# Convolution module: scaled operands instead of scaled products, four taps on another engine, earlier polyphase copies

## The chip, the cores and the metric

The kernel runs on one core of one Trainium2 chip. The metric is the device time of one execution in microseconds, as the median of several runs. A core has five engines that work side by side, each on its own list of instructions and in the order of that list: TensorE (PE: matrix products; PEld is its weight load), VectorE (DVE), ScalarE (ACT), GpSimd (POOL) and SyncE (SP), which here only issues DMA transfers. Semaphores make an instruction wait for another engine's or for a transfer; what stands behind a waiting instruction on the same engine waits too.

## The reference

Two decoder layers on 512 tokens of 1024 features, in float32. The change touches only the mixer of the first layer, a causal Conformer convolution:

```
u = rms_norm(h, conv_norm_g)                      # h * g / rms(h), per token
a = u @ w_pw1 + b_pw1                             # 1024 -> 2048
u = a[..., :1024] * sigmoid(a[..., 1024:])        # gate
u = depthwise causal convolution(u, 31 taps) + dw_b
u = silu(layer_norm(u, ln_g, ln_b))
h = h + u @ w_pw2 + b_pw2
```

Behind it come a SwiGLU feed-forward block and a gated input embedding, then the second layer (differential attention, the same two blocks). None of that is changed.

## The kernel before

**Layout.** Features lie on the 128 partitions, tokens along the free axis, so the 1024 features are eight chunks of 128 x 512, numbered c = 0 to 7. Every float32 product is made of three faster ones: each operand is split into a rounded part ("hi", a cast on ACT) and its remainder ("lo", a subtraction), and `mm3` (lines 165 to 169) adds lo x hi, hi x hi and hi x lo in PSUM. A weight is loaded into `wraw` (two buffers), cast to `whi` on ACT (L160) and its remainder written to `wlo` (L162, on DVE, at some places on POOL).

**The norm.** `Norm.split` (L201, L202) splits h times the gain g without the token's factor 1/rms, so that TensorE can begin before the factor is known. The factor is formed meanwhile, spread over all partitions by a product (L277, PSUM tile `tp`) and copied to SBUF as `rb` (L249). It is applied to the products instead: per chunk DVE multiplies the gate's sum and the value's sum by `rb` (L612 and L618).

**The loop over the chunks** (lines 579 to 638). Chunk c forms two sums of 24 matmuls each, the gate `pg` and the value `pa`. DVE scales both, ACT takes the sigmoid (L613), and DVE forms the gated chunk `up` (L632, or L624 in polyphase order). Chunks 0 and 1 have their products ahead of the others, beside the start of the kernel.

**The 31 taps.** Chunks 1, 3, 5 and 6 (`PHASED`) run on TensorE in four phases: the gated chunk goes to DRAM and back (`pi`, L419 and L423), 36 small matmuls with banded matrices make the convolution (L462), `phased_out` copies the sum out of PSUM (L470, ACT), writes it to DRAM on ACT's queue (`po`, L472), reads it back in token order on SP's queue (L475), and `shift` adds a bias and a row `shrow` (L482, DVE). Chunks 0, 2, 4 and 7 run on DVE, one instruction to a tap (L518, `sc` in PSUM); some of their taps are made by ACT (L508) and added by POOL (L509). Of chunk 7, eight taps run on TensorE with diagonal matrices (L412). `BETWEEN` and `BEHIND` say which chunk's taps TensorE takes between or behind the sums of a later chunk. The row `shrow` comes from chunk 0 alone (`moments(0)`, L557 to L561): chunks 1 to 7 need it.

**The end of the convolution.** POOL adds the finished chunks up (`macc`, L575) and their squares (L571), TensorE turns the sums (L671), DVE reduces them (L693), and from there follow the layer norm, SiLU and the last product. While the last taps run, TensorE works on six of eight pieces of a product of the first layer's input embedding (`factor`, `project`), which serve as filling; the features for them are loaded and split in `pfeatures` (L360 to L362).

**Order.** A planner orders the instructions of each engine by its own estimate; `manual_schedule` pins some pieces (the start, chunk 7's taps on DVE and the end), and `issue_after` holds an instruction back until another. SBUF tiles with one tag share buffers: the operands `A0` to `A7` have one buffer each, `wk` has four, `wraw` two, `whi` and `wlo` four.

Of the kernel before, what the change touches and what calls it, by code (L numbers as in the profile page):

```python
# [13 lines left out]
F32R = mybir.dt.float32r  # L14
AF = mybir.ActivationFunctionType
ALU = mybir.AluOpType
# [4 lines left out]
P = 128  # L21
S = 512
D = 1024
NC = D // P
# [27 lines left out]
CUTS = 2  # L52


PE_TAPS = (0, 0, 0, 0, 0, 0, 0, 8)
POOL_TAPS = (10, 0, 11, 0, 11, 0, 0, 7)


# [33 lines left out]
def trunk(ctx, tc, xT, xtok, pT, wts, diag, dww, vec, rel, onehot, lamv, out):  # L92
# [9 lines left out]
    def sb(shape, tag, bufs, dt=F32):  # L102
        uid[0] += 1
        return pool.tile(shape, dt, tag=tag, name=f"{tag}_{uid[0]}", bufs=bufs)
# [17 lines left out]
    def col(name, i=0):  # L122
        a, _ = VEC[name]
        return vt[:, a + i : a + i + 1]
# [15 lines left out]
    t = tp()  # L140
# [49 lines left out]
    def both(t):  # L190
        return t[:, 0], t[:, 1]
# [12 lines left out]
    class Norm:  # L204
# [41 lines left out]
        def rows(self):  # L246

            r = sb([P, S], "rb", 1)
            last_rows[0] = A.copy(r, spread(self.dg))  # L249
            return r  # L250

    last_v = [None]
    last_pow = [None]
# [20 lines left out]
    def spread(dg):  # L274
        t = tp()
        if not isinstance(dg, tuple):
            last_spread[0] = T.matmul(t, ones, dg, start=True, stop=True)  # L277
            return t
        for i, d in enumerate(dg):
            T.matmul(t, ones_r, d, start=i == 0, stop=i == 1)  # L280
        return t
# [99 lines left out]
    accs = {}  # L381
    last_tap = [None]
    outs = {}
    shifts = []
    last_part = [None]
    outer = []
# [2 lines left out]
    def half(w):  # L389
        acc = mm()  # L390
        for k in range(NC):
            mm3(acc, wpart(w, k), norm.u[k], k == 0, k == NC - 1)
        return acc
# [73 lines left out]
    def phased_out(c):  # L467

        o = big()
        A.copy(o, accs[c])  # L470
        d = dram.tile([P, S], F32, tag=f"po{c}", name=f"po{c}")
        outs[c] = nc.scalar.dma_start(d, o)  # L472
        both_ = sb([P, 2, S], f"B{c}", 1)
        for g in range(NPH):
            nc.sync.dma_start(  # L475
                both_[g * FG : (g + 1) * FG, 1].rearrange("p (r n) -> p r n", r=NPH),
                bass.AP(d.tensor, d.offset + g * P, [[S, FG], [FG * S, NPH], [1, P]]),
            )
        tok = "p (n r) -> p n r"

        def shift():
            V.scalar_tensor_tensor(  # L482
                both_[:, 0].rearrange(tok, r=NPH), both_[:, 1].rearrange("p (r n) -> p n r", r=NPH), col("dw_b", c),
                shrow.rearrange(tok, r=NPH), ALU.add, ALU.add,
            )
            y[c] = both_[:, 0]

        if c < NC - 3:
            shift()
        else:  # L490
            shifts.append(shift)

    def other_taps(c, behind=None):
        if c in PHASED:
            return phased_out(c)
        up, acc = ups[c], accs[c]
        alone = c in ALONE
        tap = lambda j: up[:, j : j + S]
        a, b = PE_TAPS[c], PE_TAPS[c] + POOL_TAPS[c]
        pacc = wk()  # L500
        for j in range(a, b):
            if j == a:
                with tc.issue_after(outs[5].ins) if alone else nullcontext():
                    A.activation(pacc, tap(j), AF.Identity, scale=wt(c, j), bias=col("dw_b", c))
            else:
                pr = sb([P, S], f"C{2 + j % 2}", 2)
                with tc.issue_after(outs[6 if j == b - 1 else 5].ins) if alone else nullcontext():
                    A.activation(pr, tap(j), AF.Copy, scale=wt(c, j))  # L508
                last_part[0] = G.tensor_tensor(pacc, pacc, pr, ALU.add)  # L509
        yc = sb([P, 2, S], f"B{c}", 1)  # L510
        if c == 0:
            sums["acc"] = yc[:, 1]
        yc = yc[:, 0]
        sum_ = sc() if alone else acc

        def taps(js):
            for j in js:
                V.scalar_tensor_tensor(sum_, tap(j), wt(c, j), sum_, ALU.mult, ALU.add)  # L518

        if alone:  # L520
            with tc.manual_schedule(engines={V.engine}):
                V.scalar_tensor_tensor(sum_, tap(b), wt(c, b), shrow, ALU.mult, ALU.add)
                taps(range(b + 1, b + 3))
                shifts[0]()
                moments(NC - 3)
                taps(range(b + 3, KW - 2))
                shifts[1]()
                outer.append(weight(eng=G, after=(last_part[0], None)))
                taps(range(KW - 2, KW))
                moments(NC - 2)  # L530
                outer.append(weight(eng=G, after=(last_sq[0], None)))
                V.tensor_tensor(yc, sum_, pacc, ALU.add)
                V.tensor_tensor(yc, acc, yc, ALU.add)
                y[c] = yc
                moments(c)
            return
        with tc.issue_after(behind.ins) if behind else nullcontext():
            if c == 0:
                V.tensor_scalar(sum_, tap(b), wt(c, b), None, ALU.mult)
            else:  # L540
                V.scalar_tensor_tensor(sum_, tap(b), wt(c, b), shrow, ALU.mult, ALU.add)
        taps(range(b + 1, KW))
        V.tensor_tensor(yc, sum_, pacc, ALU.add)
        y[c] = yc
# [34 lines left out]
    for c in range(NC):  # L579
# [18 lines left out]
        if 0 < c < NC - 1:  # L598
            late = ((first_gate, last_rows[0]),) * 2 if c == 1 else ((None, None),) * 2
            pairs.append(tuple(weight(after=i) for i in late)[::-1])  # L600
            pair_loads.append(loaded[0])
        if c == 1:
            ph = pfeatures(0, [(sb([P, S], t, 2, F32R), sb([P, S], t, 2, F32R)) for t in ("wth", "wtl")])
        if c > 0:
            pg = half(wg) if c > 1 else g1
            for k in BETWEEN[c]:
                pe_taps(k)
            pa = half(wa) if c > 1 else a1
            for k in BEHIND[c]:
                pe_taps(k)  # L610
        tg, ta = big(), big()
        V.tensor_tensor(tg, pg, rb, ALU.mult)  # L612
        gated = A.activation(tg, tg, AF.Sigmoid, bias=col("b_pw1", 8 + c))  # L613
        if c == NC - 1:

            with tc.issue_after(gated.ins):
                A.activation(powers[:, 24:32], vt[:, :8], AF.Silu)
        scaled = V.tensor_tensor(ta, pa, rb, ALU.mult)  # L618
        if c == 0:
            first_gate = scaled  # L620
        if c in PHASED:
            up = big()
            phases, tok = "p (r n) -> p n r", "p (n r) -> p n r"
            formed = V.scalar_tensor_tensor(  # L624
                up.rearrange(phases, r=NPH), ta.rearrange(tok, r=NPH), col("b_pw1", c),
                tg.rearrange(tok, r=NPH), ALU.add, ALU.mult,
            )
            phased_in(c, up)
        else:
            up = ups[c] = sb([P, S + PAD], "C0", 2)  # L630
            G.memset(up[:, :PAD], 0.0)
            V.scalar_tensor_tensor(up[:, PAD:], ta, col("b_pw1", c), tg, ALU.add, ALU.mult)  # L632
# [950 lines left out]
```

## Time and profile before

| | |
|---|---|
| Time, median of 3 runs | 1237.82 us (1237.47 to 1237.89) |
| Time of the profiled execution | 1238.28 us, its span 1236.3 us |
| TensorE busy | 1224.5 us, 99% of the span |
| VectorE busy | 880.1 us, 71% |
| ScalarE busy | 625.1 us, 51% |
| GpSimd busy | 474.3 us, 38% |
| Granted TensorE clock | 0.999 |
| Convolution stage | from the start to about 160 us |

The profile's times are microseconds from the start of the span of one profiled execution. A row of the timeline gives the start, the length, the engine, the line and operation, the tile written and the tiles read, the sizes, how many instructions it merges (x) and, in brackets, the idle time just before and what ended it. Instructions on DVE and ACT follow each other a little faster than their length, since the end of one overlaps the start of the next; the distance from start to start is what one costs in a dense stretch. Busy time of TensorE is not time at its peak.

### The profile page before, as it was taken

How to read it: one execution, taken by the hardware profiler on the slowest of the kernel's cores; microseconds unless marked ns; L12 is line 12 of the kernel's file. 1: busy time of each engine (PE TensorE's matmuls, PEld its weight loads, DVE VectorE, ACT ScalarE, POOL GpSimd, SP SyncE). 2: the span in 40 equal slices, each digit the busy share in tenths (PEclk: the TensorE clock that was granted, in tenths of full speed). 3: DMA queues.
4: the chain of work that ended last, by engine and by line, in shares of the span. 5: the costliest groups of instructions: out<-in, count | busy, mean ns of one | idle time of the engine just before them, and what ended most of it. 6: DMA issues, size and time to landing. Idle time of an engine off the chain costs nothing.

```text
span 1236.3 us, 18296 instructions
## 1 busy us (share of the span) xinstructions
PE 1224.5 (99%) x7011; PEld 1072.4 (87%) x7011; DVE 880.1 (71%) x1251; ACT 625.1 (51%) x1099; POOL 474.3 (38%) x355
## 2 busy tenths in 40 slices
PE   9999999999999999999999999999999999999998
PEld 7888688888998899888788888888889998999887
DVE  5889866975895479547767776747966884588545
ACT  6563464533553255434657777735534552455432
POOL 0594813024670464133436636131026640562220
PEclk9999999999999999999999999999999999999999
DMA  8664323333333322334423321142243333233331
GB/s 328 224 209 144 106 68 110 93 106 119 93 96 119 102 86 73 116 105 153 125 85 105 99 86 53 56 150 85 90 132 90 100 120 108 80 103 86 105 99 69
DMA packets 50019, 138.44 MB, mean 112 GB/s; under 512 B 5731, under 2 KB 10851, under 8 KB 49932
## 3 DMA queue, kind: packets, MB, share of 16 engines
q1 hardware_dynamic: 47664, 133.71, 35.1%
q10 hardware_dynamic: 2268, 3.57, 1.0%
q8 instruction: 55, 0.90, 0.3%
q14 instruction: 32, 0.26, 0.1%
HBM read 130.94 MB, written 6.31 MB: 111 GB/s over the span
## 4 chain that ended last, share of the span: by engine, by line
PE 84%; DVE 7%; DMA 4%; issue 3%; ACT 1%; POOL 1%; SPq 0%; ACTq 0%; DVEq 0%; POOLq 0%
PE mm L167 26%; PE mm L168 26%; PE mm L169 26%; DMA wraw<-in_wts 2%; DVE sc L518 2%; PE mm L1282 1%; DVE wlo L162 1%; PE sc L1242 1%; PE tp L1269 1%; PE sc L1239 1%; PE sc L462 1%; DMA B<-po 1%; DVE wlo L863 1%; POOL wk L509 0%; PE tp L1190 0%
## 5 line engine op out<-in xcount | busy, mean ns | idle before, releaser
L160 ACT CAST whi<-wraw 128x1024 fp32r<-128x1024 f32 (+1 forms) x139 | 141.3, 1026 | 233.4 <-PE mm L169 108.5
L167 PE MATMUL mm<-A,wlo 128*128 128x512 f32 (+1 forms) x540 | 209.7, 388 | 0.7 <-ACT A L201 0.6
L162 DVE TENSOR_TENSOR wlo<-wraw,whi 128x1024 fp32r<-128x1024 f32 (+1 forms) x132 | 167.6, 1276 | 59.7 <-ACT whi L160 59.2
L168 PE MATMUL mm<-A,whi 128*128 128x512 f32 (+1 forms) x540 | 208.6, 386 | 0.0
L169 PE MATMUL mm<-A,whi 128*128 128x512 f32 (+1 forms) x540 | 206.6, 387 | 0.1
L167 PE MATMUL mm<-B,wlo 128*128 128x512 f32 x352 | 137.0, 389 | 0.0
L168 PE MATMUL mm<-B,whi 128*128 128x512 f32 x352 | 137.0, 389 | 0.0
L224 POOL TENSOR_TENSOR acc<-acc,wk 128x512 f32<-128x512 f32 x35 | 60.9, 1741 | 195.3 <-ACT wk L223 170.8
L169 PE MATMUL mm<-B,whi 128*128 128x512 f32 x352 | 135.6, 389 | 0.0
L168 PE MATMUL mm<-C,whi 128*128 128x256 f32 x448 | 126.8, 283 | 0.0
L169 PE MATMUL mm<-C,whi 128*128 128x256 f32 x448 | 126.8, 283 | 0.0
L167 PE MATMUL mm<-C,wlo 128*128 128x256 f32 x448 | 126.8, 283 | 0.0
L863 DVE TENSOR_TENSOR wlo<-A,whi 128x1024 fp32r<-128x1024 f32 x60 | 106.7, 1789 | 20.0 <-ACT whi L862 20.0
L167 PEld LDWEIGHTS mm<-A,wlo 128*128 128x128 f32 x540 | 101.5, 188 | 22.0 <-ACT A L201 1.0
L169 PEld LDWEIGHTS mm<-A,whi 128*128 128x128 f32 x540 | 101.5, 188 | 21.3 <-DVE A L202 0.8
L168 PEld LDWEIGHTS mm<-A,whi 128*128 128x128 f32 x540 | 101.6, 188 | 20.1
L862 ACT CAST whi<-A 128x1024 fp32r<-128x1024 f32 x60 | 63.1, 1051 | 55.7 <-PE mm L169 44.7
L872 POOL TENSOR_TENSOR A<-wraw 128x512 f32<-128x512 f32 x16 | 24.7, 1541 | 170.8 <-DMA wraw<-in_wts 155.3
L168 PEld LDWEIGHTS mm<-C,whi 128*128 128x128 f32 x448 | 86.0, 192 | 0.2
L167 PEld LDWEIGHTS mm<-C,wlo 128*128 128x128 f32 x448 | 86.0, 192 | 0.2
L169 PEld LDWEIGHTS mm<-C,whi 128*128 128x128 f32 x448 | 86.0, 192 | 0.0
L872 POOL TENSOR_TENSOR A<-A 128x512 f32<-128x512 f32 x16 | 24.7, 1546 | 159.0 <-DMA A<-in_wts 156.5
(354 smaller groups left out, 3083.5 us busy)
## 6 DMA issues: line engine op xcount, KB each, us to landing
wraw<-in_wts SPq DMA_DIRECT2D x159, 512.0 KB, 3.6
A<-in_wts SPq DMA_DIRECT2D x32, 512.0 KB, 3.7
wraw<-in_wts SPq DMA_DIRECT2D x16, 384.0 KB, 3.1
D<-in_diag SPq DMA_DIRECT2D x18, 256.0 KB, 5.2
C<-in_diag SPq DMA_DIRECT2D x16, 256.0 KB, 5.2
h<-in_xT SPq DMA_DIRECT2D x8, 256.0 KB, 4.1
B<-in_xtok SPq DMA_DIRECT2D x4, 512.0 KB, 7.6
rest<-h SPq DMA_DIRECT2D x8, 256.0 KB, 2.0
```

The lines of the kernel that those rows point to most:

```text
L160: A.copy(hi[:, cut], raw[:, cut])
L162: eng.tensor_tensor(lo[:, cut], raw[:, cut], f(hi[:, cut]), ALU.subtract)
L167: T.matmul(acc, al, bh, start=first, stop=False, **kw)
L168: T.matmul(acc, ah, bh, start=False, stop=False, **kw)
L169: return T.matmul(acc, ah, bl, start=False, stop=last, **kw)
L224: self.last = self.eng.tensor_tensor(self.acc, self.acc, sq, ALU.add)
L462: last_tap[0] = T.matmul(acc[:, g * P : (g + 1) * P], w, ups[c][:, g, LEAD - m : LEAD - m + P], start=(m == 0), stop=(m == LAGS - 1),)
L518: V.scalar_tensor_tensor(sum_, tap(j), wt(c, j), sum_, ALU.mult, ALU.add)
L862: A.copy(hi, src)
L863: V.tensor_tensor(lo, src, f(hi), ALU.subtract)
L872: G.tensor_tensor(s[:, 0], r1[:, 0], r1[:, 1], ALU.add)
L1239: first = T.matmul(acc[:, :n], qs[c][:, i, cut], ks[c][:, i, 0:n], start=True, stop=False)
```

## The change

Three things are changed, all in the convolution.

- **Scaled operands.** After the products of chunks 0 and 1, `scale_again` splits h once more, now times the gain and times 1/rms: per chunk one DVE instruction (h, the gain and the spread factor in PSUM, written to `wk`), one cast on ACT into `A`, one subtraction on POOL into the other half of `A`. The tag is that of the old operands, so each new one is written when the old one's last product is done. From chunk 2 on the products need no scaling: the sigmoid reads the gate's sum in PSUM, the gated chunk is formed from the value's sum in PSUM. Chunks 0 and 1 keep the scaling. For chunk 2 the gate and the value are written as alternating products over the eight operand chunks. `pfeatures` moves from the second to the third chunk's turn.
- **Taps.** `PE_TAPS` of chunk 7 goes from 8 to 4: TensorE makes four taps less, DVE four more.
- **Polyphase copies.** For a chunk in `BETWEEN`, `phased_out` (copy, DMA to DRAM, DMAs back) is written directly behind its products; `shift` of chunks 1 and 3 stays at the later place through `back`.

The lines numbered above move: L612 is L638, L613 is L639, L618 is L645, L624 is L652, L632 is L660, L412 is L426, L462 is L476, L470 is L484, L472 is L486, L475 is L489, L482 is L496, L509 is L525, L518 is L534, L522 is L538, L671 is L699, L693 is L721. New are L258 (DVE), L260 (ACT) and L261 (POOL) of `scale_again`.

```diff
-PE_TAPS = (0, 0, 0, 0, 0, 0, 0, 8)
+PE_TAPS = (0, 0, 0, 0, 0, 0, 0, 4)
...
-            last_rows[0] = A.copy(r, spread(self.dg))
+            self.spread = spread(self.dg)
+            last_rows[0] = A.copy(r, self.spread)
             return r
+        def scale_again(self):
+            u = []
+            for c in range(NC):
+                t = wk()
+                V.scalar_tensor_tensor(t, h[c], col(self.g, c), self.spread, ALU.mult, ALU.mult)
+                hi, lo = both(sb([P, 2, S], f"A{c}", 1, F32R))
+                A.copy(hi, t)
+                G.tensor_tensor(lo, t, f(hi), ALU.subtract)
+                u.append((hi, lo))
+            return u
...
         if c < NC - 3:
-            shift()
+            back[c] = shift
         else:
             shifts.append(shift)
...
         if c in PHASED:
-            return phased_out(c)
+            if c not in outs:
+                phased_out(c)
+            return back[c]() if c in back else None
...
-        if c == 1:
+        if c == 2:
             ph = pfeatures(0, ...)
-        if c > 0:
+        if c == 2:
+            norm.u = scaled_u
+            pg, pa = mm(), mm()
+            for k in range(NC):
+                mm3(pg, wpart(wg, k), norm.u[k], k == 0, k == NC - 1)
+                mm3(pa, wpart(wa, k), norm.u[k], k == 0, k == NC - 1)
+        elif c > 0:
             pg = half(wg) if c > 1 else g1
             for k in BETWEEN[c]:
                 pe_taps(k)
+                if k in PHASED:
+                    phased_out(k)
...
-        tg, ta = big(), big()
-        V.tensor_tensor(tg, pg, rb, ALU.mult)
-        gated = A.activation(tg, tg, AF.Sigmoid, bias=col("b_pw1", 8 + c))
+        tg = big()
+        ta = big() if c < 2 else pa
+        if c < 2:
+            V.tensor_tensor(tg, pg, rb, ALU.mult)
+        gated = A.activation(tg, tg if c < 2 else pg, AF.Sigmoid, bias=col("b_pw1", 8 + c))
...
-        scaled = V.tensor_tensor(ta, pa, rb, ALU.mult)
+        if c < 2:
+            scaled = V.tensor_tensor(ta, pa, rb, ALU.mult)
         if c == 0:
             first_gate = scaled
+            scaled_u = norm.scale_again()
```

On DVE the start of the chunk loop, from the first use of the factor `rb` on, reads before (`wlo_309` and `wlo_315` are chunk 2's weights):

```order
L612 TENSOR_TENSOR big_299<-mm_194,rb_273 128x512
L618 TENSOR_TENSOR big_300<-mm_195,rb_273 128x512
L612 TENSOR_TENSOR big_332<-mm_244,rb_273 128x512
L162 TENSOR_TENSOR wlo_309<-wraw_307,whi_308 128x1024
L162 TENSOR_TENSOR wlo_315<-wraw_313,whi_314 128x1024
L632 SCALAR_TENSOR_TENSOR C_54_304<-big_300,vec_63,big_299 128x512
L618 TENSOR_TENSOR big_333<-mm_269,rb_273 128x512
L539 TENSOR_SCALAR sc_331<-C_54_304,C_31_133 128x512
```

and now, at the same place of DVE (chunk 2's weights are `wlo_349` and `wlo_355`, `wk` holds a newly scaled chunk):

```order
L638 TENSOR_TENSOR big_299<-mm_194,rb_273 128x512
L645 TENSOR_TENSOR big_300<-mm_195,rb_273 128x512
L258 SCALAR_TENSOR_TENSOR wk_304<-h_6_75,vec_63,tp_274 128x512
L258 SCALAR_TENSOR_TENSOR wk_309<-h_7_76,vec_63,tp_274 128x512
L258 SCALAR_TENSOR_TENSOR wk_314<-h_8_77,vec_63,tp_274 128x512
L258 SCALAR_TENSOR_TENSOR wk_319<-h_9_78,vec_63,tp_274 128x512
L638 TENSOR_TENSOR big_360<-mm_244,rb_273 128x512
L162 TENSOR_TENSOR wlo_349<-wraw_347,whi_348 128x1024
L162 TENSOR_TENSOR wlo_355<-wraw_353,whi_354 128x1024
L660 SCALAR_TENSOR_TENSOR C_70_344<-big_300,vec_63,big_299 128x512
L645 TENSOR_TENSOR big_361<-mm_269,rb_273 128x512
L258 SCALAR_TENSOR_TENSOR wk_324<-h_10_79,vec_63,tp_274 128x512
```

Four scalings have moved ahead of chunk 2's weight remainders; the other four follow the first gated chunk (L660). On POOL the eight new remainders (L261) stand directly behind the factor itself, ahead of chunk 0's first added tap (L509, now L525). On ACT, near the end of the loop, the copy of chunk 5's polyphase sum (`sc_1075`) and its DMA now read:

```order
L160 CAST whi_1345<-wraw_1344 128x1024
L484 COPY big_1128<-sc_1075 128x512
L639 ACTIVATE big_1213<-mm_1050,vec_63 128x512
L643 ACT_TABLE_LOAD
L643 ACTIVATE mhalf_71<-vec_63 128x8
L486 DMA po_1130<-big_1128 128x512
```

where before the sigmoid, the table load and one more weight cast (`whi_1337`) came first:

```order
L160 CAST whi_1325<-wraw_1324 128x1024
L613 ACTIVATE big_1179<-big_1179,vec_63 128x512
L617 ACT_TABLE_LOAD
L617 ACTIVATE mhalf_71<-vec_63 128x8
L160 CAST whi_1337<-wraw_1336 128x1024
L470 COPY big_1188<-sc_1050 128x512
L472 DMA po_1190<-big_1188 128x512
```

The copy has moved ahead of the sigmoid and the table load, its DMA has not: it still stands behind the table load in ACT's list.

More of the change, by code (lines that the diff above doesn't have):

```diff
@@ L383, in trunk @@
     outs = {}
+    back = {}
     shifts = []
```

## The prediction

> **What bounds the kernel now.** I read the page first, then busy time by stage, then the timeline of each engine between 25 and 146 us, where all of the change lies. The page says that TensorE is the bound:
>
> ```profile
> PE 1224.5 (99%) x7011; PEld 1072.4 (87%) x7011; DVE 880.1 (71%) x1251; ACT 625.1 (51%) x1099; POOL 474.3 (38%) x355
> PE 84%; DVE 7%; DMA 4%; issue 3%; ACT 1%; POOL 1%; SPq 0%; ACTq 0%; DVEq 0%; POOLq 0%
> ```
>
> The second row is the chain that ended last; its 7% of DVE needs a place. Two stretches of the windows view give it (per stretch: length, then busy us of PE, PEld, DVE, ACT, POOL):
>
> ```profile
> 25.85:54.20 28.35, 28.35 (x164) 24.81 (x162) 25.64 (x31) 19.45 (x26) 16.78 (x11) 1.00 0.64 207
> 121.00:146.00 25.00, 23.39 (x128) 17.73 (x129) 22.78 (x28) 11.44 (x18) 18.74 (x14) 1.00 0.44 139
> ```
>
> At the start of the chunk loop TensorE never waits; at the end of the convolution it waits, and DVE is busy for nearly all of that stretch. TensorE's waits from the loop to there are these (its timeline, the wait in brackets):
>
> ```profile
> 107.16 1.02 PE L462 MATMUL sc<-C,D 128*128 128x128 f32 x7 [0.94 <-DMA B<-po]
> 121.17 0.68 PE L462 MATMUL mm<-C,B 128*128 128x128 f32 x4 [0.26 <-DMA C<-pi]
> 144.00 0.66 PE L671 MATMUL sc<-ident,acc 128*128 128x128 f32 x4 [0.87 <-POOL acc L575]
> 145.23 0.66 PE L671 MATMUL mm<-ident,B 128*128 128x128 f32 x4 [0.57 <-POOL B L571]
> ```
>
> So two things set the end of this stage: TensorE's own work up to chunk 6's taps, and behind it DVE's list for chunk 7, whose end in this execution is the L533 row:
>
> ```profile
> 130.96 1.98 DVE L482 SCALAR_TENSOR_TENSOR B<-B,vec,shrow 128x512 f32<-128x512 f32 x1 [1.17 <-DMA B<-po]
> 132.86 8.65 DVE L518 SCALAR_TENSOR_TENSOR sc<-C,C,sc 128x512 f32<-128x512 f32 x11
> 141.43 1.17 DVE L482 SCALAR_TENSOR_TENSOR B<-B,vec,shrow 128x512 f32<-128x512 f32 x1
> 144.98 0.69 DVE L533 TENSOR_TENSOR B<-mm,B 128x512 f32<-128x512 f32 x1
> ```
>
> After 146 us neither the work nor, but for renumbering, the order changes, so what the convolution ends later or earlier is the change of the whole. The profiled execution took 1238.28 us, span 1236.3; the median is 1237.82. I sum shifts against the profiled timeline and add them to the median. 0.2% of it, about the least that a measurement of this kernel can tell from none, is 2.5 us.
>
> **Part 1, the taps.** The groups view of DVE and PE (xcount | busy, mean ns):
>
> ```profile
> L412 PE MATMUL mm<-C,D 128*128 128x512 f32 x16 | 7.0, 592 | 0.0
> L612 DVE TENSOR_TENSOR big<-mm,rb 128x512 f32<-128x512 f32 x8 | 5.5, 685 | 2.1 <-ACT rb L249 1.8 <-PE mm L169 0.3
> L618 DVE TENSOR_TENSOR big<-mm,rb 128x512 f32<-128x512 f32 x8 | 5.5, 684 | 0.1
> ```
>
> Eight taps are 16 matmuls and 7.0 us, so TensorE loses 3.5 us. But they stand between chunk 6's taps and the filling products, after which TensorE waits for POOL anyway (0.87 and 0.57 us above): alone they bring nothing, they lengthen a wait. DVE's eleven taps took 8.65 us, 0.786 each; four more are 3.1 us, and these lie on the path, between the two L482 of the fence above.
>
> **Part 2, products that need no scaling.** Of L612 and L618, six each go. They follow each other at 0.60 us (25.88 to 27.09 below holds two), so DVE gains 12 x 0.60 = 7.2 us, spread over the loop. Against that stand eight scalings at 0.60, all at its beginning. L560 is the nearest row for one: the same operation with one operand in PSUM, 0.69 us long like L612.
>
> ```profile
> 67.46 0.69 DVE L560 SCALAR_TENSOR_TENSOR B<-tp,B 128x512 f32<-128x512 f32 x1 [2.42 <-ACT shrow L559]
> ```
>
> In all DVE has 8 x 0.60 + 3.1 - 7.2 = 0.7 us more to do: about even. What matters is when.
>
> **Part 3, TensorE's wait at chunk 2.** Now (timeline of DVE, then PE and ACT):
>
> ```profile
> 25.88 0.69 DVE L612 TENSOR_TENSOR big<-mm,rb 128x512 f32<-128x512 f32 x1 [1.84 <-ACT rb L249]
> 27.09 0.68 DVE L612 TENSOR_TENSOR big<-mm,rb 128x512 f32<-128x512 f32 x1
> 27.68 2.35 DVE L162 TENSOR_TENSOR wlo<-wraw,whi 128x1024 fp32r<-128x1024 f32 x2
> 29.87 0.39 PE L167 MATMUL mm<-A,wlo 128*128 128x512 f32 x1
> 54.16 0.48 PE L167 MATMUL mm<-A,wlo 128*128 128x512 f32 x1
> 29.06 1.34 ACT L613 ACTIVATE big<-big,vec 128x512 f32<-128x512 f32 x2
> 31.51 2.56 ACT L508 ACTIVATE C<-C,C 128x512 f32<-128x512 f32 x4
> 33.97 0.60 ACT L361 CAST wth<-wraw 128x512 fp32r<-128x512 f32 x1
> 40.80 1.05 ACT L160 CAST whi<-wraw 128x1024 fp32r<-128x1024 f32 x1 [2.10 <-DMA wraw<-in_wts]
> ```
>
> Chunk 2's first product came at 29.65 (one matmul, 0.227 us, before the 29.87 row) and its weights' remainders were done at 30.0. In the new order four scalings come ahead of these remainders: factor 25.88, two scaled products to 27.09, four scalings to 29.5, one scaled product to 30.1; the first remainder ends at 31.3. TensorE waits 1.7 us there. Then each operand chunk needs its cast (ACT: first sigmoid 29.06 to 29.73, casts every 0.5 us from there) and its remainder on POOL. POOL alone needs this long for one, and with DVE beside it this happens:
>
> ```profile
> 37.89 1.30 POOL L362 TENSOR_TENSOR wtl<-wraw,wtl 128x512 fp32r<-128x512 f32 x1
> 98.38 1.73 POOL L575 TENSOR_TENSOR acc<-acc,B 128x512 f32<-128x512 f32 x1
> 100.08 2.27 POOL L571 TENSOR_TENSOR B<-B,wk 128x512 f32<-128x512 f32 x1
> 97.22 1.76 DVE L541 SCALAR_TENSOR_TENSOR sc<-C,C,shrow 128x512 f32<-128x512 f32 x1
> 98.89 2.31 DVE L162 TENSOR_TENSOR wlo<-wraw,whi 128x1024 fp32r<-128x1024 f32 x1
> L162 DVE TENSOR_TENSOR wlo<-wraw,whi 128x1024 fp32r<-128x1024 f32 x13 | 18.6, 1435 | 2.8 <-ACT whi L160 2.8
> ```
>
> The DVE remainder of 98.89 takes 2.31 us, not 1.17 as in the pair of 27.68, and ends 1.1 us after POOL's 98.38 row; POOL's next ends 1.15 us after it. They took turns: each stood still until the other was done. I take turns as the price here, since the weight remainders, L660 and L261 all read two SBUF tiles; the mean of all thirteen, the last row's 1.435 us, would be the milder reading. The Trainium skill has a rule on this (SBUF — State Buffer, "Who interferes with whom"): a VectorE instruction with two SBUF inputs and a GpSimd one that reads SBUF exclude each other for the whole instruction; the trace agrees in the 2.31 us, and by the rule the wait below is 5.0 us, by the mean 3.0.
>
> By turns: first weight remainder to 31.2; POOL's first 31.1 to 32.4; second weight remainder to 33.5; POOL's second to 34.65; L660 to 35.25; POOL's third to 36.45, fourth 37.7. TensorE, six matmuls to an operand chunk but in the order of the program (gate of chunks 0 to 3, then value), waits 0.6 us for the first remainder, 1.55 for the second, 1.1 for the third. The rest is covered: the eleven value products (2.5 us) hide the fourth. ACT's next four casts stand behind four taps (L508's kind, 2.56 us, from L660's 35.25) and a weight cast (1.05): 38.8; TensorE comes there at 40.1. The other remainders come at 41.0, 43.3, 45.6, 46.9, and products of chunk 3 fill in. Sum 1.7 + 0.6 + 1.55 + 1.1 = 5.0 us: what began at 54.16 begins near 59.2. Bounds: 1.7 us if only the weight waits, 6.5 if POOL takes the first turn and L660 and with it ACT's casts slip by another 1.5.
>
> The 0.94 us wait at 107 (a chunk's way through DRAM, no later than now) is then covered. So chunk 7's products end, instead of at 120.9, at 120.9 - 0.94 + 5.0 = 124.9; chunk 6's taps, behind which this row began,
>
> ```profile
> 129.28 1.02 PE L412 MATMUL mm<-C,D 128*128 128x512 f32 x2
> ```
>
> at 129.3 - 0.94 - 0.26 + 5.0 = 133.1. With 3.5 us of taps gone, filling ends about where it did.
>
> **Part 4, the copies.** Before, chunk 5's copy was late though its taps were done at 115.2:
>
> ```profile
> 115.19 0.47 PE L167 MATMUL mm<-A,wlo 128*128 128x512 f32 x1
> 121.90 0.58 ACT L470 COPY big<-sc 128x512 f32<-128x512 f32 x1
> 122.51 0.33 ACTq L472 DMA_DIRECT2D po<-big  x1
> 119.12 1.28 ACT L617 ACT_TABLE_LOAD   x1
> ```
>
> The way from that DMA's issue to the L482 at 130.96 is 8.45 us. Now the taps end at 115.2 - 0.94 + 5.0 = 119.3; copy 0.6, sigmoid 0.7, table load with its little activation 1.8 stand ahead of the DMA: issue near 122.3, only 0.2 us earlier. The matrices' loads that ran beside it come about 1 us earlier too, so I take 7.5 us of way: 129.8. DVE reaches that place sooner: L660 at 124.9, three taps, 128.1. So it waits for the copy, then 1.1 to 1.9 us for it (both lengths are in the rows), 15 taps 11.8: the last L496 begins near 143.1, where L482 began at 141.43. Chunk 6's data, with taps ended at 133.1 and 9 us for copy and way, is there at 142.2. Behind it two taps and three small steps are as before; one reduction moves ahead of L549's kind (+0.6) and is missing behind it.
>
> **Sum.** 143.1 - 141.43 = +1.7 us: 1237.8 + 1.7 = 1239.5. TensorE's taps are gained and the wait at chunk 2 eats them.
>
> **Rivals.**
> *A, the forecast (0.48).* Wait 5.0 at chunk 2, end +1.7. With the wait's upper bound 6.5 it is +3.2, so a quarter of this case lies beyond 2.5.
> *B, chunk 0 late (0.30, slower).* Chunk 0's added taps on POOL and its last step on DVE stand here before:
>
> ```profile
> 32.29 3.13 POOL L509 TENSOR_TENSOR wk<-wk,C 128x512 f32<-128x512 f32 x2 [8.98 <-ACT C L508]
> 60.38 0.69 DVE L543 TENSOR_TENSOR B<-sc,wk 128x512 f32<-128x512 f32 x1
> ```
>
> Now POOL's eight remainders stand ahead; the taps and the two features' remainders begin at 46.9 instead of 32.3, and eleven steps of 1.3 end at 61.2. The features hold the two `wraw` buffers until 52, so the weights behind them, of which DVE forms three remainders before its last step, come some 4 us apart from 54 on. I estimate L543 6 us later and L560's kind (67.46) 3 to 5 later; everything on DVE needs `shrow` from it. For it: DVE had only 2.42 us of idle there, and chunk 3's copy still stands behind POOL-paced taps on ACT. Against it: 7.2 us of scaling gone. It decides once DVE reaches chunk 7 later than 124.9; I find 123.4, so 1.5 us of room. With 2.2 us beyond it and A's 1.7: 1237.8 + 3.9 = 1241.7.
> *C, no taking turns (0.14).* POOL and DVE slow each other only as the mean of L162 suggests. Then the wait is about 3.0, chunk 5's copy goes out 2.0 us earlier and the end is -0.3: 1237.5.
> *D, operands in time (0.08, faster).* If the wait stays under 1 us, DVE has chunk 7 near 120, chunk 5's data at 125, and the last L496 at 138: -3.4, so 1234.4. The weight remainder behind four scalings speaks against it.
> That the copies are not "right behind" is in A already: one DMA hardly moves.
>
> **Numbers.** Faster by over 0.2%: D, 0.08. Slower: B's most (0.28) and a quarter of A (0.12), 0.40. Within: 0.52. The range runs from between D and C, 1235.5, to beyond B with the wait's upper bound, 1243.5; A alone is 1238 to 1241.
>
> **What would show it.** On TensorE, waits of about 5 us between 29 and 41, first for `wlo`, then for POOL's `A`; the first 0.94 us wait at 107 gone. On DVE, L496 of chunk 5 at about 130 after a wait on its DMA, the last at 143. Wrong: no waits for `A` (C or D), or DVE reaching L660 of chunk 7 late with TensorE long done (B). TensorE's busy time should fall by 3.5 us in any case.

## The result, and the profile after

The changed kernel takes 1240.70 us (median of 20 runs, 1238.97 to 1242.67), the kernel before 1237.86 in the same comparison: ratio 1.0023, 95% interval 1.0016 to 1.003, so +2.8 us. The profiled execution took 1239.85 us, its span is 1238.1. The page, first busy time, then the chain that ended last:

```profile
PE 1224.2 (99%) x7003; PEld 1072.0 (87%) x7003; DVE 876.2 (71%) x1251; ACT 628.7 (51%) x1107; POOL 487.8 (39%) x363
PE 92%; DVE 3%; issue 1%; DMA 1%; ACT 1%; POOL 1%; SPq 0%; ACTq 0%; DVEq 0%
```

TensorE has eight matmuls less and is busy only 0.3 us less, not 3.5; its share of the chain rose from 84% to 92%. The two places where it went are the ones that the prediction looked at. First the start of the loop (timeline of TensorE, then GpSimd and VectorE):

```profile
30.99 0.47 PE L167 MATMUL mm<-A,wlo 128*128 128x512 f32 x1 [1.65 <-DVE wlo L162]
32.04 0.50 PE L169 MATMUL mm<-A,whi 128*128 128x512 f32 x1 [0.35 <-POOL A L261]
34.24 0.79 PE L169 MATMUL mm<-A,whi 128*128 128x512 f32 x1 [1.24 <-POOL A L261]
60.31 0.48 PE L167 MATMUL mm<-A,wlo 128*128 128x512 f32 x1
29.67 7.45 POOL L261 TENSOR_TENSOR A<-wk,A 128x512 fp32r<-128x512 f32 x4 [7.08 <-ACT A L260]
25.19 0.69 DVE L638 TENSOR_TENSOR big<-mm,rb 128x512 f32<-128x512 f32 x1 [1.88 <-ACT rb L250]
29.62 3.44 DVE L162 TENSOR_TENSOR wlo<-wraw,whi 128x1024 fp32r<-128x1024 f32 x2
```

The factor was used 0.69 us earlier than in the profile of before (25.19, there 25.88), as executions differ; a time of this profile is therefore worth 0.7 us more when it is held against the profile of before. What began at 54.16 begins at 60.31: 6.15 later, 6.8 with that. But the waits listed are 3.24 us. The rest is in the windows (per stretch: length, busy us of PE, PEld, DVE, ACT and POOL, granted TensorE clock, DMA share, GB/s):

```profile
32.00:34.00 2.00, 0.96 (x3) 0.48 (x3) 2.00 (x2) 0.00 (x0) 2.00 (x1) 0.73 0.61 236
34.00:36.00 2.00, 1.71 (x4) 0.90 (x4) 2.00 (x4) 1.18 (x2) 2.00 (x3) 0.50 0.83 246
36.00:38.00 2.00, 2.00 (x5) 1.61 (x6) 2.00 (x4) 2.00 (x4) 1.12 (x1) 0.50 0.41 158
38.00:40.00 2.00, 2.00 (x7) 1.57 (x6) 2.00 (x3) 2.00 (x4) 1.09 (x1) 0.56 0.02 8
40.00:42.00 2.00, 2.00 (x11) 1.63 (x10) 2.00 (x3) 2.00 (x4) 2.00 (x2) 1.00 0.34 131
```

From about 33 to 40 us the granted clock is halved (by these rows for 6.8 us in all): five matmuls in the 2 us from 36, eleven in the 2 us from 40. TensorE counts as busy in it, which is why its busy time did not fall. Second, the end of the convolution on VectorE and ScalarE, and TensorE's first row behind the eighth chunk's products:

```profile
66.23 0.69 DVE L559 TENSOR_TENSOR B<-sc,wk 128x512 f32<-128x512 f32 x1
73.17 0.69 DVE L576 SCALAR_TENSOR_TENSOR B<-tp,B 128x512 f32<-128x512 f32 x1 [2.42 <-ACT shrow L575]
105.51 1.15 DVE L496 SCALAR_TENSOR_TENSOR B<-B,vec,shrow 128x512 f32<-128x512 f32 x1 [4.16 <-DMA B<-po]
125.97 0.75 DVE L660 SCALAR_TENSOR_TENSOR C<-mm,vec,big 128x512 f32<-128x512 f32 x1 [0.66 <-ACT wk L582]
130.74 1.13 DVE L496 SCALAR_TENSOR_TENSOR B<-B,vec,shrow 128x512 f32<-128x512 f32 x1 [0.63 <-DMA B<-po]
131.78 11.82 DVE L534 SCALAR_TENSOR_TENSOR sc<-C,C,sc 128x512 f32<-128x512 f32 x15
143.52 1.11 DVE L496 SCALAR_TENSOR_TENSOR B<-B,vec,shrow 128x512 f32<-128x512 f32 x1
96.72 0.73 ACT L524 ACTIVATE C<-C,C 128x512 f32<-128x512 f32 x1 [0.65 <-POOL wk L525]
97.35 0.57 ACT L484 COPY big<-sc 128x512 f32<-128x512 f32 x1
121.52 0.33 ACTq L486 DMA_DIRECT2D po<-big  x1
121.64 1.28 ACT L643 ACT_TABLE_LOAD   x1
125.71 0.49 PE L476 MATMUL mm<-C,B 128*128 128x128 f32 x3
146.03 0.66 PE L699 MATMUL sc<-ident,acc 128*128 128x128 f32 x4 [1.86 <-POOL acc L591]
```

The first chunk's sum is 5.9 us later (66.23, before 60.38), `shrow` 5.7 later (73.17, before 67.46). VectorE stands 4.16 us for the fourth chunk's copy, which was made only at 97.35, behind taps that wait for GpSimd. VectorE's tile for the eighth chunk (125.97) and TensorE's last product for it (the one ahead of the row of 125.71, done at about 125.9) then come together: two chains, equally late. (The row of 125.97 names ScalarE's step behind the fifth chunk as what ended the wait of 0.66 us; TensorE was done only 0.1 us earlier.) The last addition is at 143.52, 2.1 us after the 141.43 of before, or 2.8 counted from the use of the factor, which is the measured difference.

### The profile page after: what moved, and what is told of

The parts are those of the page before. It is cut to its first block, busy times and chain, and to the rows that moved or that the text cites. A ratio compares the mean times of both kernels' runs of the same rounds, so it can differ in the third digit from the quotient of the medians.

```text
span 1238.1 us, 18303 instructions
## 1 busy us (share of the span) xinstructions
PE 1224.2 (99%) x7003; PEld 1072.0 (87%) x7003; DVE 876.2 (71%) x1251; ACT 628.7 (51%) x1107; POOL 487.8 (39%) x363
## 4 chain that ended last, share of the span: by engine, by line
PE 92%; DVE 3%; issue 1%; DMA 1%; ACT 1%; POOL 1%; SPq 0%; ACTq 0%; DVEq 0%
PE mm L167 28%; PE mm L169 28%; PE mm L168 28%; PE sc L476 2%; PE mm L1310 1%; DVE sc L534 1%; PE sc L1270 1%; PE sc L1267 1%; PE tp L1297 1%; PE tp L1218 1%; DVE wlo L891 1%; POOL A L261 1%; DMA h<-in_xT 0%; DMA po<-big 0%; DVE wk L974 0%
## 5 line engine op out<-in xcount | busy, mean ns | idle before, releaser
L891 DVE TENSOR_TENSOR wlo<-A,whi 128x1024 fp32r<-128x1024 f32 x60 | 103.4, 1731 | 21.3 <-ACT whi L890 21.2
```

The costliest lines, as they stand in the source:

```text
L891: V.tensor_tensor(lo, src, f(hi), ALU.subtract)
```

## The experiments

All were timed against the kernel before on the same chip; its median lay between 1237.40 and 1238.10 us. Ratios are to it, with the 95% interval.

**The third wait and the clock.** Fillers at the waits of the third chunk (`fill` chains matmuls into a spare bank; chunk 0's later steps are held behind these products so that the order stays):

```diff
+FILL = (7, 1, 6, 4)
...
+            behind = fill(FILL[0], last_a1)
             for k in range(NC):
...
+                    m = T.matmul(pg, ah, bh, start=False, stop=False)
+                if k < 3:
+                    behind = fill(FILL[1 + k], m)
```

> The changed kernel with eighteen 512-column matmuls added into a spare bank, so that TensorE works instead of waiting at the third chunk: 7 behind the second chunk's products, then 1, 6 and 4 behind the first two products of the third chunk's first three operands (at 0.227 us each about 1.6, 0.2, 1.4 and 0.9 us). The theory of the clock (the three short waits, 1.65 + 0.35 + 1.24 us in the profile of the changed kernel, are what lets the granted clock fall to 0.50 from 34 to 40 us, and this costs about 3 us more): the clock stays at 1.00 there, the third chunk's taps or products end some 2.5 to 3 us earlier than in the changed kernel, and the eighth chunk's products end at about 123 us instead of 125.7; the time falls by only 0.4 to 1.5 us, to 1239.2 to 1240.3, since VectorE comes to the eighth chunk at 125.3 anyway. If the low clock came from something else (the other engines' load, or chance): 0.50 in the same stretch with the fillers too, and 1240.4 to 1241.

Measured 1241.52 us, 1.0028 [1.0019, 1.0037]. The clock (windows) of the filled kernel, the first use of the factor, and what began at 60.31 in the changed kernel (timeline):

```profile
34.00:36.00 2.00, 2.00 (x10) 1.35 (x8) 2.00 (x3) 0.97 (x2) 2.00 (x2) 1.00 0.78 205
25.37 0.69 DVE L659 TENSOR_TENSOR big<-mm,rb 128x512 f32<-128x512 f32 x1 [1.84 <-ACT rb L254]
59.06 0.48 PE L171 MATMUL mm<-A,wlo 128*128 128x512 f32 x1
105.86 1.16 DVE L501 SCALAR_TENSOR_TENSOR B<-B,vec,shrow 128x512 f32<-128x512 f32 x1 [3.90 <-DMA B<-po]
125.79 0.75 DVE L682 SCALAR_TENSOR_TENSOR C<-mm,vec,big 128x512 f32<-128x512 f32 x1
```

So the waits did lower the clock: with work in them it stays at 1.00. But TensorE is only 1.3 us earlier (59.06 for 60.31), since the remainders' pace stays, and nothing of it reaches the end: VectorE still waits 3.90 us and comes at 125.79, without a wait for TensorE. The expected gain of 0.4 to 1.5 us did not appear; the median is 0.8 us above that of the changed kernel, but the two intervals overlap. Counted from the first use of the factor, this step of TensorE is 5.4 us later than before here, and 6.8 in the changed kernel. In two runs below (the scaling alone, the addition held back) the same waits lowered the clock for 3.4 us instead of 6.8, and it is 6.1 us later. So the late operands are worth 5.4 us at most (the fillers may add to it), and the low clock 0.7 to 1.4 on top, as the execution has it.

**The fourth chunk instead of the third.** Products 0 to 2 are scaled as before; the eight scalings go behind the third chunk's weights, and `pfeatures` is back at the second chunk's turn:

```diff
-        if c == 2:
+        if c == 3:
+            scaled_u = norm.scale_again(lo_chunk2)
             norm.u = scaled_u
...
-        if c < 2:
+        if c < 3:
```

> The changed kernel with the operands scaled from the fourth chunk on instead of the third; the third chunk's two products are multiplied by the factor as before, and the eight scalings stand behind the third chunk's weights on VectorE. The theory of the clock and the waits: by 45 us, when the fourth chunk begins, all scaled operands are there, TensorE doesn't wait, its clock stays at 1.00 in each stretch of 2 us between 25 and 60, and the first chunk's VectorE taps are no later than in the changed kernel (66.2) by over 1 us. The forecast's own rival then holds: the 3.5 us of the four taps come off TensorE, the end lies at 1236 to 1238. If what costs is only that VectorE has more before the eighth chunk (its scalings, 4.8 us, less the 6 products' 6 us and the four taps' 3.1 us): 1239.5 to 1241, with VectorE's first step of the eighth chunk at 125 us again.

Measured 1239.74 us, 1.0011 [1.0002, 1.002]. Neither theory as written: the operands are in time, but the scalings push the second chunk's input back, TensorE waits 3.83 us for its way through DRAM, and its clock falls again:

```profile
44.59 1.62 PE L480 MATMUL sc<-C,D 128*128 128x128 f32 x6 [3.83 <-DMA C<-pi]
46.00:48.00 2.00, 2.00 (x11) 2.00 (x11) 2.00 (x4) 2.00 (x5) 2.00 (x2) 0.50 0.79 219
```

**The parts alone.** The copies (only the hunks on `phased_out` and `back`), the scaling (without these and with eight taps), the taps (`PE_TAPS` alone):

> The kernel before with the third part of the change alone: the polyphase chunks' sums copied right behind their products, the addition of the result left where the others stand; nothing scaled, eight taps on TensorE. By the forecast's steps the fourth and sixth chunk's copies cost nothing and start earlier, the wait of 0.94 us at 107 may go: 1237.0 to 1238.0. If the early copies are what hurts (a later chunk's work pushed back on ScalarE): above 1238.5.

> The changed kernel with eight taps on TensorE and with the polyphase copies where the kernel before has them: the scaled operands alone. By the theory of waits and low clock TensorE stands 6 us later at the fourth chunk as in the changed kernel; its eight taps cost 3.5 us more on TensorE behind that, VectorE has 3.1 less: where the eighth chunk's products bound, 1241 to 1243. By the theory that VectorE's four taps and its late arrival at the eighth chunk are what costs: 1237.5 to 1239.

> The kernel before with the change's first part alone: four of the eighth chunk's eight taps go from TensorE to VectorE. By the forecast's step (3.1 us more on VectorE between the last two additions, nothing gained on TensorE, which waits there for GpSimd anyway) the last layer norm begins 2 to 3 us later: 1239.9 to 1241.0. If VectorE's time there is covered by the filling products: 1237.3 to 1238.3.

Measured: copies 1244.73 us, 1.0053 [1.004, 1.0065]; scaling 1242.49, 1.0038 [1.0024, 1.0052]; taps 1240.67, 1.002 [1.0011, 1.0029]. Alone they cost 6.9, 4.7 and 2.6 us, together 2.8: the parts do not add. The copies alone (VectorE, TensorE):

```profile
99.05 1.14 DVE L483 SCALAR_TENSOR_TENSOR B<-B,vec,shrow 128x512 f32<-128x512 f32 x1 [4.22 <-DMA B<-po]
100.11 1.18 DVE L629 SCALAR_TENSOR_TENSOR big<-big,vec,big 128x512 f32<-128x512 f32 x1
110.69 1.62 PE L463 MATMUL sc<-C,D 128*128 128x128 f32 x6 [5.42 <-DMA C<-pi]
```

The fourth chunk's copy starts 6.4 us earlier (89.95, before 96.32), but the planner moves its addition on VectorE further still, ahead of the sixth chunk's input (L629), behind which it stood before. The addition waits 4.22 us for its data, the input goes out late, and TensorE stands 5.42 us. The scaling alone is late on TensorE (VectorE waits for the eighth chunk's product; its last addition, at 141.32, is no later than before, but TensorE ends its filling only at 147.7, and VectorE's sums wait 2.36 us for that):

```profile
126.21 0.75 DVE L658 SCALAR_TENSOR_TENSOR C<-mm,vec,big 128x512 f32<-128x512 f32 x1 [3.87 <-PE mm L169]
```

The taps alone lengthen VectorE's stretch between the last two additions, as the forecast had it, from 10.5 to 13.3 us, while TensorE idles and its clock falls (timeline, then windows):

```profile
128.01 1.67 DVE L482 SCALAR_TENSOR_TENSOR B<-B,vec,shrow 128x512 f32<-128x512 f32 x1
141.34 1.08 DVE L482 SCALAR_TENSOR_TENSOR B<-B,vec,shrow 128x512 f32<-128x512 f32 x1
143.82 1.11 PE L671 MATMUL sc<-ident,acc 128*128 128x128 f32 x4 [5.91 <-POOL acc L575]
144.00:146.00 2.00, 1.89 (x8) 1.25 (x8) 1.72 (x3) 0.00 (x0) 2.00 (x2) 0.50 0.00 0
```

But the stretch begins earlier there, in part since VectorE need not wait for the sixth chunk's copy. This execution used the factor 1.1 us earlier than that of before (24.80); counted from it, the last addition is 1.0 us late and the first step of the layer norm on VectorE (L708, 152.25, before 150.28) 3.0: about two thirds of the loss come in the stage with the low clock, behind the wait of 5.91 us. That the taps cost less in the changed kernel, where TensorE is late and can use its 3.5 us, is argued from this and not tried by itself.

**One copy alone.** The early copy for the sixth chunk only (`if k == 5:` in place of `if k in PHASED:`, in the kernel before):

> The kernel before with the early copy for the sixth chunk alone; the second and fourth chunk's copies stay. If the loss of all three copies together (+6.9) came from the fourth chunk's addition, which then stood ahead of the sixth chunk's input on VectorE and held it for 4.2 us: nothing of it here, VectorE's wait of 1.17 us for the sixth chunk's copy gone, 1236.6 to 1237.9. If early copies cost in themselves: 1239 or more.

Measured 1242.34 us, 1.0028 [1.0016, 1.0041]. Its eleven runs fall into two groups: five with a mean granted clock of 0.999 or 1.0 took 1238.45 to 1241.05, six with 0.996 or 0.997 took 1242.34 to 1245.86. The expectation (1236.6 to 1237.9) failed in both. The wait for the sixth chunk's copy is gone, as expected; in the profiled execution, which took 1245.76 us and so is one of the second group, the loss sits in a place that the copy doesn't touch:

```profile
147.00 0.77 PE L167 MATMUL mm<-wth,wlo 128*128 128x512 f32 x1 [5.29 <-DVE B L536]
```

A filling product on TensorE waits for VectorE's last addition (L536), which reads a PSUM tile of the same pool. That the tiles' turn had shifted is argued, not shown, and how long this wait is in the first group no profile shows. (The clock of this execution is at 0.50 from 146.1 to 152.9.) That an edit of one part moves other things with it is shown; so the three parts' prices alone include such moves.

**The two late chains.** VectorE's 4.16 us are taken away by holding the fourth chunk's addition behind six taps:

```diff
+        taps(range(b + 1, b + 6))
+        if c == 4:
+            with tc.issue_after(own_tap[0].ins):
+                back[3]()
+        taps(range(b + 6, KW))
```

> The changed kernel with one move on VectorE: the addition of the fourth chunk's copy stands behind the first six taps of the fifth chunk instead of ahead of five of them, as it did in the kernel before; the copy itself goes out as early as in the changed kernel. Theory of two chains (VectorE's 4.16 us of waiting for that copy, and TensorE's late products, end within a microsecond of each other at the eighth chunk): VectorE is done with the fifth chunk near 121, then waits some 3 to 4 us for the eighth chunk's value product, which ends at about 125.7 as before; the sixth chunk's copy may be earlier; the time gains at most 0.8, 1239.9 to 1240.9. Theory that VectorE's wait alone was the cost: 1236.5 to 1237.5.

> Both chains eased: the addition moved as in the run beside it, and the eighteen filling matmuls that kept TensorE's clock at 1.00. In the filled kernel the first taps on TensorE (of the second chunk) began at 51.1 instead of 52.4, so the low clock had cost 1.3 us net of the fillers' own time. Theory of two chains: the eighth chunk's products end 1.0 to 1.5 us earlier, 124.3 to 124.8, VectorE takes them at once, and the time is 1238.5 to 1239.7, less than either edit alone gives. If a third thing sets the end (the copies of the sixth and seventh chunk): no better than the addition alone.

Measured: 1239.80 us, 1.0012 [1.0003, 1.0021] with the addition alone. VectorE, and TensorE's step of 60.31:

```profile
107.91 1.14 DVE L496 SCALAR_TENSOR_TENSOR B<-B,vec,shrow 128x512 f32<-128x512 f32 x1
122.67 0.69 DVE L563 TENSOR_TENSOR B<-sc,wk 128x512 f32<-128x512 f32 x1
125.75 0.75 DVE L664 SCALAR_TENSOR_TENSOR C<-mm,vec,big 128x512 f32<-128x512 f32 x1 [2.39 <-PE mm L169]
60.09 0.48 PE L167 MATMUL mm<-A,wlo 128*128 128x512 f32 x1
```

The wait for the copy is gone, the fifth chunk is done 2 us earlier, and the eighth chunk's tile comes 0.2 us earlier: the time goes into a wait for TensorE. That is the theory of two chains; the 0.9 us that are gained (the two intervals overlap) come right behind, where the sixth chunk's addition begins at 128.98 without a wait instead of 130.74. A second move helped there: the DMA of that copy was issued at 120.84, right behind the copy, and not at 121.52, as the sigmoid ended. With the fillers as well it was 1240.98 us, 1.0021 [1.0013, 1.003], not the 1238.5 to 1239.7 expected: there TensorE also waits 1.7 us for ScalarE's copy of the first chunk's sum (`moments(0)`), whose product stands too early in its new order, and the eighth chunk's tile comes at 127.29. So this run does not decide.

**What the scaling itself costs.** The changed kernel without `scale_again`. It leaves the factor 1/rms out of chunks 2 to 7, so it shows a time and computes something else:

```diff
-            norm.u = scaled_u
...
-            scaled_u = norm.scale_again()
```

> The changed kernel without its eight scalings, their casts and remainders: from the third chunk on the products are formed from the operands that aren't scaled and aren't multiplied by the factor either, so that part of the computation is left out; copies and taps as in the changed kernel. It shows what the scaling itself costs. If the scalings' late operands are what brings the loss: TensorE doesn't wait at the third chunk, its clock stays at 1.00, the taps of the second chunk begin near 40 (before: 40.8, the changed kernel: 52.4 behind the fourth chunk's gate products), VectorE is done with the fifth chunk before 119, the eighth chunk's products end near 120.5 instead of 125.7, and the time falls by 4 to 6 us, to 1235 to 1237. If the loss sits in the last stage (four taps more on VectorE, GpSimd's last sums): at most 1.5 us faster, 1239.2 to 1240.5.

Measured 1235.79 us, 0.9983 [0.9974, 0.9992]: 4.9 us less than the changed kernel. TensorE waits for nothing between 20 and 137, its clock is 1.00, the eighth chunk's products end at 119.3 (timeline of TensorE; VectorE):

```profile
119.30 0.38 PE L476 MATMUL mm<-C,B 128*128 128x128 f32 x2
98.60 1.14 DVE L496 SCALAR_TENSOR_TENSOR B<-B,vec,shrow 128x512 f32<-128x512 f32 x1 [5.20 <-DMA B<-po]
119.57 0.75 DVE L658 SCALAR_TENSOR_TENSOR C<-mm,vec,big 128x512 f32<-128x512 f32 x1 [1.16 <-PE mm L169]
```

VectorE's wait for the fourth chunk's copy is even longer here (5.20 us) and costs nothing. So the loss is the scalings' (their late operands and the work that they bring to VectorE, ScalarE and GpSimd; the first chunk's sum is done at 58.00 here, not at 66.23); the copy's wait counts only together with them. Which of these it is, the next versions tell. The second chunk's taps began at 45.96, not near 40 as expected, since other products stand ahead of them.

**A version that beats both.** Scaled operands from the fourth chunk on, the scalings behind the second chunk's input (`formed`), the addition behind six taps, with eight, four and six taps on TensorE:

```diff
+            scaled_u = norm.scale_again(formed)
             norm.u = scaled_u
...
-PE_TAPS = (0, 0, 0, 0, 0, 0, 0, 4)
+PE_TAPS = (0, 0, 0, 0, 0, 0, 0, 6)
```

> Scaled operands from the fourth chunk on, with the eight scalings behind the second chunk's input on VectorE (in the earlier run they stood ahead of it and TensorE waited 3.8 us for that input), early copies, the fourth chunk's addition behind six taps, and all eight taps on TensorE. By the theory of TensorE's waits: no wait over 1 us between 25 and 60, clock 1.00, the eighth chunk's products end by 122, VectorE (the fifth chunk done near 122) takes them at once, some 2 us before the kernel before (124.5); the last stage, as in the kernel before, then ends 1 to 2 us earlier: 1236 to 1237.2, faster than both kernels. If GpSimd (eight remainders among its taps) makes the first chunk late: 1238 to 1240, with VectorE's fifth chunk done after 124.

> The run beside it with four taps on TensorE and four more on VectorE. If VectorE sets the last stage once nothing is late (as the four taps alone cost the kernel before 2.6 us): 1.5 to 3 us slower than the run beside it, TensorE waiting some 4 to 6 us for GpSimd's last sum at a clock that falls to 0.50 behind it. If TensorE is still late at the eighth chunk (as in the changed kernel, where eight taps with late copies gave 1242.5): up to 2 us faster than it.

> The fourth-chunk version with six taps on TensorE, between the two before it. With four, TensorE stood 1.71 and 0.57 us behind its filling work (from 137.65) and its clock then fell to 0.50 from about 140.1 to 143.5; with eight, VectorE waited 1.79 us for the seventh chunk's copy and TensorE ended its filling last. If VectorE's and TensorE's last stretches are what the number of taps shares out: filling ends 1.75 us later than with four, at 139.4, VectorE's last addition begins 1.1 us earlier, at 135.75, when the copy lands; TensorE waits under 0.7 us there, its clock stays at 1.00 from 140 to 144, and the time is 1233.3 to 1234.5. If the seventh chunk's copy alone sets that end: as with four or eight, 1234.8 to 1236.4.

Measured: eight 1236.40 us, 0.9987 [0.9978, 0.9995]; four 1234.84, 0.9979 [0.9971, 0.9988]; six 1233.01, 0.9964 [0.9952, 0.9976]. With four taps, the scalings on VectorE, TensorE's clock over the stage that was lost, and its end:

```profile
31.55 1.16 DVE L666 SCALAR_TENSOR_TENSOR big<-big,vec,big 128x512 f32<-128x512 f32 x1
32.54 5.33 DVE L262 SCALAR_TENSOR_TENSOR B<-h,vec,tp 128x512 f32<-128x512 f32 x8
30.00:60.00 30.00, 30.00 (x170) 26.23 (x169) 29.43 (x35) 18.73 (x30) 27.72 (x20) 1.00 0.75 235
119.89 0.74 DVE L674 SCALAR_TENSOR_TENSOR C<-mm,vec,big 128x512 f32<-128x512 f32 x1
139.36 0.66 PE L713 MATMUL sc<-ident,acc 128*128 128x128 f32 x4 [1.71 <-POOL acc L599]
140.59 0.69 PE L713 MATMUL mm<-ident,B 128*128 128x128 f32 x2 [0.57 <-POOL B L595]
142.00:143.00 1.00, 1.00 (x6) 1.00 (x5) 0.80 (x2) 0.10 (x1) 0.85 (x1) 0.50 0.00 0
```

No wait between 30 and 60, full clock, and the eighth chunk's tile at 119.89 instead of 125.97. The scalings themselves are all still there, and the first chunk's sum and the first step with `shrow` are as late as in the changed kernel (66.65 and 73.28, there 66.23 and 73.17). So neither the work nor the late first chunk explains the loss, but where the scalings stand. The comparison that changes little else (the third chunk's products are scaled as before, `pfeatures` is back at the second chunk's turn) is the run with the addition held back, which also has four taps: 1239.80 there, 1234.84 here. With eight taps the time was as expected; VectorE waits 1.79 us for the seventh chunk's copy and TensorE's filling ends last. That four were faster than eight came out as the second theory's number, but not by its reason, as TensorE was not late at the eighth chunk; and the intervals of four and eight overlap, as do those of four and six. Only six against eight is clear of the noise. Six fit between (TensorE, VectorE, in an execution of 1234.57 us):

```profile
139.11 0.60 PE L713 MATMUL sc<-ident,acc 128*128 128x128 f32 x4
134.92 2.00 DVE L500 SCALAR_TENSOR_TENSOR B<-B,vec,shrow 128x512 f32<-128x512 f32 x1
142.00:144.00 2.00, 2.00 (x8) 1.03 (x6) 1.26 (x5) 0.00 (x0) 0.54 (x1) 1.00 0.47 135
```

Neither engine waits there and the clock stays at 1.00. The median, 0.3 us below the 1233.3 to 1234.5 expected, is 4.4 us less than that of the kernel before.

## Where the prediction was right, and which of its steps failed

The forecast was +1.7 us, 1239.5; measured +2.8, 1240.7. The way and the mechanism were right (TensorE waits at the third chunk, and through the sixth chunk's copy this reaches the last addition), the size was 1.1 us short. The change lies just beyond the 0.2%: the forecast gave 0.40 to a kernel slower by more than that, and 0.52 to a change within it. The end that it summed, the last addition, came at 143.52 where it said 143.1; but the factor was used 0.69 us earlier, so against the forecast's timeline it is 144.2. The times in brackets below are converted in this way.

- **Part 1, the taps.** Right as to VectorE's work: 15 taps took 11.82 us. The 2.6 us that the taps cost alone lie near the 3.1 forecast partly by luck, since only 1.0 of it came through the last addition and the rest in a stage with a lowered clock. Wrong as to TensorE's busy time "in any case": it fell by 0.3 us, since 6.8 us at half the clock count as busy too.
- **Part 2, about even on VectorE.** Its busy time fell by 3.9 us (880.1 to 876.2) instead of rising by 0.7. What mattered was when, as the part said: with the same scalings one chunk later the kernel is faster than the one before.
- **Part 3, TensorE's wait.** The order of the waits was right: first `wlo` (1.65 us, forecast 1.7), then GpSimd's remainders (0.35 and 1.24, forecast 0.6 and 1.55; the third, forecast at 1.1, shows no wait). Taking turns was right: four remainders in 7.45 us, 1.86 each where one alone took 1.30, and the two weight remainders 3.44 us instead of 2.35. The Trainium skill's rule (SBUF — State Buffer, "Who interferes with whom") agrees with these rows. One reading was off by a matmul: the row at 29.87 is itself the third chunk's first product, which makes the first wait 0.2 us shorter. The mis-sized term is the sum: 5.0 us forecast, 6.8 measured. With the clock held at 1.00 by the filled kernel it was 5.4, so most of the difference is the low clock, for which no step allowed.
- **Part 4, the copies.** Two errors cancelled here, which is luck. The sixth chunk's taps ended at 120.4 (121.1) and not at 119.3, as the wait was 1.8 us longer; and the step "copy, sigmoid, table load stand ahead of the DMA" was wrong: the DMA was issued at 121.52, ahead of the table load at 121.64, though ScalarE's list has it behind. So it went out at 122.2 in the forecast's timeline, where the forecast had 122.3. The term that was then too small is the way, 9.2 us and not the 7.5 taken (with the taps alone it was 7.4 at most, in the filled kernel 9.4). The addition began at 130.74 (131.4), forecast 129.8. The wait of 0.94 us at 107 was covered, as said.
- **What the forecast held as a rival.** B came beside A, not in its place: the first chunk's sum was 5.9 us late (6.5; forecast 6) and the first step with `shrow` 5.7 (6.4; forecast 3 to 5), and VectorE came to the eighth chunk at about 125.3 (126.0), past the 124.9 from which B was to decide. But that lateness is not enough by itself, as the versions from the fourth chunk on have it too and are faster. The missing part of its chain is the fourth chunk's addition, which waited 4.16 us; the forecast said that this copy stands behind GpSimd-paced taps, but gave VectorE's wait for it no price. As both chains ended together, taking one away gained 0.9 us (the addition held back) or nothing (the fillers).
- **C and D** fell with the waits. What D said of operands in time, 1234.4, is about what the kernel without scalings (1235.79) and the versions from the fourth chunk on (1236.40 to 1233.01) gave.

Open: how much of the copies' and of the scaling's price alone belongs to the planner's other moves, as in the run with one copy; and what decides for how long the same waits lower the clock.

## What to carry to other kernels

Price a step that feeds the busiest engine by when its first result is there, not by the work it saves: with the addition held back and four taps in both, the same scaled operands cost 1.7 us against the kernel before when they stood one chunk early, and gained 2.9 us one chunk later, behind the input that another engine was waiting for. Where two chains end together, removing either one shows almost nothing, so look at which wait takes the place of the one removed. A copy that starts earlier helps only if the step that reads it does not move ahead by more.

## What the hardware showed that was not expected

Short waits lower the granted clock, and for longer than they last. In the changed kernel it was at 0.50 for 6.8 us from 32.9 on, behind waits of 1.65 and 0.35 us and just ahead of the one of 1.24; with four taps in the last version for 3.4 us (140.1 to 143.5), behind a wait of 1.71 us and as one of 0.57 began. With single waits of 3.83, 5.42 and 5.91 us it was 6.8 us each, which began before the wait was over. The lengths of the waits alone do not decide it: with 1.69, 0.34 and 1.24 us in the run with the addition held back, at the same place as in the changed kernel, the clock fell only at 35.3 and for 3.4 us; and 1.86, 0.57 and 0.25 us at 144 to 148 in the changed kernel, like the 0.94 us of before, left it at 1.00. The Trainium skill (TensorE: Matmul & The Clock Gate, "HAM oscillation — how this bites in real kernels") gives as the rule that gaps over about 3.4 us bring the clock down to half; the half agrees with the 0.50 here, the bound does not, since no single gap of the first two cases reached 1.8 us.
